# The feed-forward input projection of a decoder layer as seven products of quarters, with its gates passed through DRAM

## The chip, the cores and the metric

The kernel runs on one core of one Trainium2 chip. The metric is the device time of one execution in microseconds (us). Engines are named as in the profile: PE (TensorE) multiplies matrices, with its weight loads counted apart as PEld; DVE (VectorE) does element-wise work; ACT (ScalarE) casts and activation functions; POOL (GpSimd) element-wise work and DMA issues; SP (SyncE) only issues DMAs. Each engine works through its own instructions strictly in order.

## The reference

One layer of a decoder, 1024 tokens of width 1024, in float32. A token mixer (three branches, an output projection) comes first and is not touched. What matters here is the end:

```python
mix = hybrid_mixer(x, ...)                                  # ends in merged @ w_out
x = layer_norm(DEEPNORM_ALPHA * x + mix, ln1_g, ln1_b)
h1, h3 = split(x @ w_ffn_in, 2)                             # w_ffn_in: 1024 x 5632
ffn = (silu(h1) * h3) @ w_ffn_out                           # w_ffn_out: 2816 x 1024
x = layer_norm(DEEPNORM_ALPHA * x + ffn, ln2_g, ln2_b)
```

## The kernel before

Every float32 operand is held as two float32r parts, hi (a cast on ACT) and lo (the value minus hi, on DVE), and every product is three matmuls: hi by hi, hi by lo and lo by hi. A matmul has a 128x128 block of one operand stationary and 512 columns of the other moving, and adds into a bank of PSUM (`acc`, eight banks in this stage).

Weights come through `WeightStream` (`W`): a chunk of 512 KB is loaded by SP's queue into `w_raw` (L82, two buffers), split by ACT (`w_hi`, L96) and DVE (`w_lo`, L97; two buffers each) and used by a step of matmuls (L179). `W.run` emits the steps in order and yields after some matmuls; `run_steps` then runs one closure of the list `later`, so that norms and transposes are placed between matmuls. A scheduler sets the final order on each engine from what is emitted and its own estimates.

The output projection leaves the sums of a row tile (128 tokens) in PSUM; tiles 0 to 3 are done first, then 4 and 5, then 6 and 7. `ln1_front` adds the residual (`residual`, L914, DVE) and queues the norm: statistics (L924, L927 on DVE), a square root (L928, ACT), a reciprocal (L929), a scaling (L932) and the multiplication by ln_g (L935) on DVE, the addition of ln_b (L936) on POOL, and a store of the row to `x1_dram` on POOL's queue (L966), from which it is read again as the residual of the second norm (`res`, L908). Then come the transposes: `split_transpose` puts four 128x128 blocks of a row tile into PSUM by PE (L250), and ACT and DVE split them (L252, L253) into `x1h` and `x1l`, one pair of tiles for each half of the tokens.

The feed-forward goes over the halves of the tokens, `th` = 0 and 1. `ffn_in(th)` takes the 22 blocks j of 128 hidden columns; for each it projects h1 (columns j*128) and h3 (columns 2816 + j*128): 8 blocks of the contraction by 3 matmuls each. ACT takes the silu of h1 from PSUM (L990), DVE multiplies by h3 from PSUM (L995), and the gate is split into `gh` (L996, ACT) and `gl` (L997, DVE), which stay in SBUF. `ffn_out(th)` multiplies them with the output weights, for two halves of 512 columns and, for each, all 22 blocks j and 4 row tiles, 3 matmuls each; the second norm follows through `later`, so that the norm of th = 0 lies beside the projection of th = 1.

## Time and profile before

| what | value |
|---|---|
| three runs | 2314.52, 2318.84, 2319.31 us; median 2318.84 |
| span of the profiled execution | 2313.5 us; time around it isn't on the page, the median is 5.3 us above the span |
| busy | PE 98%, PEld 83%, DVE 54%, ACT 39%, POOL 12% of the span |
| output projection | until about 1571 us of the span |
| input projection, th = 0 and th = 1 | 1571 to 1814 and 1937 to 2180 us |
| output product, th = 0 and th = 1 | 1814 to 1937 and 2180 to 2304 us |

A row of a timeline gives the start, the time, the engine, the line of the kernel, the operation and out<-in; several like operations without a gap are one row with their count, and in brackets stands how long the engine was idle before and what ended that. A row of DMA issues gives the count, the size and the median time from issue to landing.

### The profile page before, as it was taken

How to read it: one execution, taken by the hardware profiler on the slowest of the kernel's cores; microseconds unless marked ns; L12 is line 12 of the kernel's file. 1: busy time of each engine (PE TensorE's matmuls, PEld its weight loads, DVE VectorE, ACT ScalarE, POOL GpSimd, SP SyncE). 2: the span in 40 equal slices, each digit the busy share in tenths (PEclk: the TensorE clock that was granted, in tenths of full speed). 3: DMA queues.
4: the chain of work that ended last, by engine and by line, in shares of the span. 5: the costliest groups of instructions: out<-in, count | busy, mean ns of one | idle time of the engine just before them, and what ended most of it. 6: DMA issues, size and time to landing. Idle time of an engine off the chain costs nothing.

```text
span 2313.5 us, 29381 instructions
## 1 busy us (share of the span) xinstructions
PE 2270.6 (98%) x11441; PEld 1919.2 (83%) x11441; DVE 1248.0 (54%) x2370; ACT 910.6 (39%) x1674; POOL 274.0 (12%) x267
## 2 busy tenths in 40 slices
PE   8989999999999999999999999999999999999998
PEld 6777888998888888788888888888888887888886
DVE  5789888777867778611232332475333226333335
ACT  4664766655656555511221221323232213323222
POOL 1332122212121222000000000021000002000001
PEclk9999999999999999999999999999999999999999
DMA  4123123122222233411231221343333334333333
GB/s 137 55 69 100 47 64 78 48 47 63 46 64 46 54 77 113 138 59 46 75 99 46 73 83 46 114 155 123 96 96 100 105 114 128 99 100 92 114 119 114
DMA packets 232651, 199.08 MB, mean 86 GB/s; under 512 B 8704, under 2 KB 196160, under 8 KB 232512
## 3 DMA queue, kind: packets, MB, share of 16 engines
q1 hardware_dynamic: 207360, 137.90, 19.7%
q0 software_dynamic: 10752, 32.03, 5.6%
q10 hardware_dynamic: 14400, 27.27, 3.6%
q8 instruction: 90, 1.47, 0.3%
q14 instruction: 49, 0.40, 0.1%
HBM read 161.52 MB, written 25.17 MB: 81 GB/s over the span
## 4 chain that ended last, share of the span: by engine, by line
PE 90%; DVE 6%; ACT 1%; issue 1%; DMA 1%; SPq 0%; DVEq 0%; ACTq 0%
PE acc L179 79%; PE o L179 4%; PE s L179 4%; PE pt L516 3%; DVE xc L359 1%; DVE w_lo L97 1%; DMA xin<-in_x_dram 0%; DVE xc L356 0%; PE pt L250 0%; DVE m L398 0%; DVE pt_l L521 0%; DVE r L932 0%; DVE p L557 0%; DVE gate L397 0%; DVE p L600 0%
## 5 line engine op out<-in xcount | busy, mean ns | idle before, releaser
L96 ACT CAST w_hi<-w_raw 128x1024 fp32r<-128x1024 f32 x233 | 245.2, 1052 | 797.3 <-PE acc L179 752.7
L97 DVE TENSOR_TENSOR w_lo<-w_raw,w_hi 128x1024 fp32r<-128x1024 f32 x195 | 248.0, 1272 | 492.4 <-ACT w_hi L96 488.3
L179 PE MATMUL acc<-xh,w_hi 128*128 128x512 f32 x1056 | 419.4, 397 | 5.0 <-DVE kl L501 2.0
L179 PE MATMUL acc<-xl,w_hi 128*128 128x512 f32 x1056 | 416.4, 394 | 0.0
L179 PE MATMUL acc<-xh,w_lo 128*128 128x512 f32 x1056 | 415.5, 393 | 0.0
L179 PE MATMUL acc<-x1h,w_lo 128*128 128x512 f32 x704 | 274.3, 390 | 2.7 <-DVE w_lo L97 2.7
L179 PE MATMUL acc<-x1h,w_hi 128*128 128x512 f32 x704 | 274.6, 390 | 0.0
L179 PE MATMUL acc<-x1l,w_hi 128*128 128x512 f32 x704 | 273.9, 389 | 0.0
L179 PEld LDWEIGHTS acc<-xh,w_hi 128*128 128x128 f32 x1056 | 199.7, 189 | 44.6 <-ACT xr L348 2.6
L179 PEld LDWEIGHTS acc<-xh,w_lo 128*128 128x128 f32 x1056 | 199.6, 189 | 39.3
L179 PEld LDWEIGHTS acc<-xl,w_hi 128*128 128x128 f32 x1056 | 200.0, 189 | 37.6
L936 POOL TENSOR_TENSOR r<-r,ln_b 128x1024 f32<-128x1024 f32 x15 | 40.6, 2714 | 1300.6 <-DVE r L935 1275.8
L520 ACT CAST pt_h<-pt 128x512 fp32r<-128x512 f32 (+3 forms) x256 | 124.9, 500 | 92.1 <-PE pt L516 87.2
L179 PEld LDWEIGHTS acc<-x1h,w_lo 128*128 128x128 f32 x704 | 132.1, 188 | 31.1 <-DVE w_lo L97 3.5
L521 DVE TENSOR_TENSOR pt_l<-pt,pt_h 128x512 fp32r<-128x512 f32 (+3 forms) x256 | 144.4, 572 | 19.7 <-ACT pt_h L520 17.5
L179 PEld LDWEIGHTS acc<-x1h,w_hi 128*128 128x128 f32 x704 | 132.2, 188 | 27.2
L179 PEld LDWEIGHTS acc<-x1l,w_hi 128*128 128x128 f32 x704 | 132.2, 188 | 27.1
L179 PE MATMUL acc<-yh,w_hi 128*128 128x512 f32 x384 | 149.4, 389 | 0.0
L179 PE MATMUL acc<-yl,w_hi 128*128 128x512 f32 x384 | 149.4, 389 | 0.0
L179 PE MATMUL acc<-yh,w_lo 128*128 128x512 f32 x384 | 149.4, 389 | 0.0
L516 PE MATMUL pt<-ident,p 128*128 128x128 f32 x816 | 128.3, 276 | 2.1 <-DVE pt_l L521 1.4
L179 PE MATMUL o<-pt_h,v 128*128 128x256 f32 (+1 forms) x464 | 117.4, 275 | 2.5 <-DVE yp L510 1.8
(278 smaller groups left out, 4069.4 us busy)
## 6 DMA issues: line engine op xcount, KB each, us to landing
w_raw<-in_w_ffn_in_dram SPq DMA_DIRECT2D x88, 512.0 KB, 3.6
w_raw<-in_w_in_dram SPq DMA_DIRECT2D x76, 512.0 KB, 3.7
w_raw<-in_w_ffn_out_dram SPq DMA_DIRECT2D x47, 512.0 KB, 3.6
w_raw<-in_w_branch_dram SPq DMA_DIRECT2D x24, 512.0 KB, 3.9
yraw<-y_dram ACTq DMA_DIRECT2D x48, 256.0 KB, 3.4
w_raw<-in_w_out_dram SPq DMA_DIRECT2D x12, 512.0 KB, 3.5
kh<-kh POOLq DMA_DIRECT2D x20, 256.0 KB, 5.9
kl<-kl POOLq DMA_DIRECT2D x20, 256.0 KB, 6.4
```

The source lines that it names most:

```text
L96: self.nc.scalar.copy(hi, raw)
L97: self.lo_engine.tensor_sub(lo, raw, hi.bitcast(F32))
L179: pe.matmul(o, a, b, start=start, stop=stop, skip_group_check=True)
L359: dve.scalar_tensor_tensor(xc, xr[:, 1 + j:1 + j + S], vec[:, j * 8 + ct:j * 8 + ct + 1], xc, op0=OP.mult, op1=OP.add)
L516: pe.transpose(pt[:, i * P:(i + 1) * P], b, ident)
L520: act.copy(dst_h, v)
L521: dve.tensor_sub(dst_l, v, dst_h.bitcast(F32))
L936: (pool if cols == D else dve).tensor_add(r[:, sl], r[:, sl], lnp["b"][:, sl])
```

## The change

The input projection is done by one level of Strassen's scheme (in Winograd's form). The activations are cut into four quarters, a00 and a01 (tokens 0 to 511; first and second half of the width), a10 and a11 (tokens 512 to 1023), and so are the weights of a block j: rows in two halves, columns h1 and h3. In place of eight products of quarters there are seven, of the operands a00, a01, a11 and the sums s1 = a10 + a11, s2 = s1 - a00, s3 = a00 - a10 and s4 = a01 - s2, with the weights' own quarters or their sums t1 to t4.

- `ln1_front` forms the activation sums on DVE for tiles 4 to 7 (L1000 to L1006), writing over the rows of the norm. The row's store to `x1_dram` is now issued by SP (L983); for tiles 6 and 7 DVE adds ln_b. `run_steps` runs two closures per piece from tile 4 on. Transposes: 112 in place of 64.
- `front_step` does the a00 and a01 products of the first four blocks (`NA` = 4), which need only tokens 0 to 511; the first result is copied out (`p1`), then a01's is added in the same bank and silu taken.
- `prep(j)` loads the two weight chunks of a block (L1083), forms t1 to t4 on POOL (`wsum`, L1088) and splits them, and one quarter, on ACT and DVE (`wsplit`, L1098 and L1099; the first chunk whole for j of 4 and above).
- `pair(j)` does the products of a block, for both halves of the tokens together: a00, s2, s1, s3, a01, s4, a11 in banks ba, bb, bc, bd; s4 goes on in bc and a11 in bd, after DVE has taken what stood there (L1154, L1158). DVE adds and multiplies to the two gates, which POOL's queue stores to `g_dram` (L1168, L1175).
- `load_g` reads the gates back, 22 for th = 0 on SP's queue and 22 for th = 1 on POOL's (L1203), and splits them for `ffn_out`, into the room of s2, s3 and s4 (j below 12) or new tiles. Both `ffn_out` follow each other; the norm of th = 0 lies beside `ffn_out(1)`.

The core of the diff:

```diff
-    def run_steps(g):
+    def run_steps(g, n=1):
         for _ in g:
-            if later:
-                later.pop(0)()
+            for _ in range(n):
+                if later:
+                    later.pop(0)()
...
-        halves, rest = norm_ops(r, D, lambda sl: pool.dma_start(x1_dram[tt], r))
+        halves, rest = norm_ops(r, D, lambda sl: sync.dma_start(x1_dram[tt], r), dve if tt >= 6 else pool)
...
+            def sums0():
+                s1 = lnr.tile([P, HALF], F32, tag="s1", bufs=4, name="s1")
+                rows_["s1", i] = s1
+                dve.tensor_add(s1, r[:, :HALF], r[:, HALF:])
+                dve.tensor_sub(r[:, :HALF], rows_[i][:, :HALF], r[:, :HALF])
+
+            def sums1():
+                lo, hi = rows_[i][:, :HALF], rows_[i][:, HALF:]
+                dve.tensor_sub(lo, rows_["s1", i], lo)
+                dve.tensor_sub(hi, hi, lo)
+            later.extend([sums0, sums1])
...
+    def product(bank, op, bh, bl, start):
+        ah, al = ops[op]
+        for k in range(4):
+            wh, wl = bh[:, k * P:(k + 1) * P], bl[:, k * P:(k + 1) * P]
+            mm(bank, wh, ah[:, k, :], start and k == 0, False)
+            mm(bank, wh, al[:, k, :], False, False)
+            mm(bank, wl, ah[:, k, :], False, k == 3)
...
+    def front_step(j):
+
+        def f(hi, lo):
+            bank = acc8.tile([P, HALF], F32, tag="acc", name="acc")
+            got = []
+            for q in range(2):
+                sl = slice(q * HALF, (q + 1) * HALF)
+                yield from product(bank, L_OPS[q], hi[:, sl], lo[:, sl], q == 0)
+                got.append(front_evac(bank, q))
+            front[j] = got
...
+    def wsum(j, n, a, b, op):
+        t = sring.tile([P, HALF], F32, tag="t", bufs=3, name="t")
+        pool.tensor_tensor(t, a, b, op=op)
+        raws[j, n] = t
...
+        def p1():
+            wsum(j, "t1", b(0, 1), b(0, 0), OP.subtract)
+            wsum(j, "t2", b(1, 1), raws[j, "t1"], OP.subtract)
...
+        def p5():
+            wsum(j, "t3", b(1, 1), b(0, 1), OP.subtract)
+            wsplit(j, "t3", raws[j, "t3"])
+        def p6():
+            wsplit(j, "b11", b(1, 1))
+            wsum(j, "t4", b(1, 0), raws[j, "t2"], OP.subtract)
+            wsplit(j, "t4", raws[j, "t4"])
...
+        yield from product(bb, "s2", *parts.pop((j, "t2")), True)
+        u2 = temp()
+        dve.tensor_add(u2, p1, bb)
+        yield from product(bc, "s1", *parts.pop((j, "t1")), True)
+        v = temp()
+        dve.tensor_add(v, u2, bc)
+        yield from product(bd, "s3", *parts.pop((j, "t3")), True)
+        dve.tensor_add(v, v, bd)
+        if j >= NA:
+            yield from product(ba, "a01", b0h[:, HALF:], b0l[:, HALF:], False)
+            silu = front_evac(ba, 1)
+        yield from product(bc, "s4", *parts.pop((j, "b11")), False)
+        g = temp()
+        dve.tensor_add(g, u2, bc)
+        dve.tensor_mul(g, g, silu)
+        pool.dma_start(g_dram[0, j], g)
+        yield from product(bd, "a11", *parts.pop((j, "t4")), False)
+        g = temp()
+        dve.tensor_add(g, u2, bd)
+        act.activation(g, g, AF.Silu)
+        dve.tensor_mul(g, g, v)
+        pool.dma_start(g_dram[1, j], g)
...
+    def load_g(th, j):
...
+        raw = l.bitcast(F32)
+        (pool if th else sync).dma_start(raw, g_dram[th, j])
+        act.copy(h, raw)
+        dve.tensor_sub(l, raw, h.bitcast(F32))
...
+    for f in prep(0):
+        f()
+    for j in range(HT):
+        nxt = prep(j + 1) if j + 1 < HT else []
+        drain(pair(j, lambda n: nxt[n]() if nxt else None))
+    srS.close()
+    for j in range(12):
+        load_g(0, j)
```

The order on the engines, before and after. On DVE, from the last norm work on tile 5 to the residual of tile 6; before:

```order
L932 TENSOR_SCALAR r<-r,sm 128x1024
L935 TENSOR_TENSOR r<-r,ln_g 128x1024
L914 SCALAR_TENSOR_TENSOR r<-res,acc 128x512 x2
L924 BN_STATS stats<-r 128x6
L914 SCALAR_TENSOR_TENSOR r<-res,acc 128x512
L924 BN_STATS stats<-r 128x6 x2
L914 SCALAR_TENSOR_TENSOR r<-res,acc 128x512
L927 BN_AGGR sm<-stats 128x2
L924 BN_STATS stats<-r 128x6
```

After (`s_...` is a tile's s1, `r<-r` at L1001 and L1006 a sum written over a row):

```order
L939 TENSOR_TENSOR r<-r,ln_g 128x1024
L1001 TENSOR_TENSOR r<-r 128x512
L1000 TENSOR_TENSOR s_13891<-r 128x512
L1005 TENSOR_TENSOR r<-s_13857,r 128x512
L1006 TENSOR_TENSOR r<-r 128x512
L1001 TENSOR_TENSOR r<-r 128x512
L1005 TENSOR_TENSOR r<-s_13891,r 128x512
L1006 TENSOR_TENSOR r<-r 128x512
L918 SCALAR_TENSOR_TENSOR r<-res,acc 128x512 x2
L928 BN_STATS stats<-r 128x6
L918 SCALAR_TENSOR_TENSOR r<-res,acc 128x512
L928 BN_STATS stats<-r 128x6 x2
```

Seven sums of tiles 4 and 5, and one more above the piece, now stand ahead of the residual of tile 6 (L918).

On PE, from the output projection (`wo_h`, `mh`) on; before, all of the projection of the first half follows:

```order
L179 MATMUL acc<-wo_h,mh 128x512 x2
L179 MATMUL acc<-wo_l,mh 128x512 x2
L179 MATMUL acc<-wo_h,ml 128x512 x2
L179 MATMUL acc<-x1h,w_hi 128x512
L179 MATMUL acc<-x1l,w_hi 128x512
L179 MATMUL acc<-x1h,w_lo 128x512
L179 MATMUL acc<-x1h,w_hi 128x512
```

After, the same place is followed by the front products (`oph` and `opl` are the parts of a00, a01, a11 or s1), and their end by the last transposes and pair 0, whose weight parts are called `ph` and `pl`:

```order
L180 MATMUL acc<-oph,w_lo 128x512
L180 MATMUL acc<-oph,w_hi 128x512
L180 MATMUL acc<-opl,w_hi 128x512
L180 MATMUL acc<-oph,w_lo 128x512
L251 MATMUL pt<-ident,r 128x128 x14
L180 MATMUL acc<-s2h,ph 128x512
L180 MATMUL acc<-s2l,ph 128x512
L180 MATMUL acc<-oph,ph 128x512
L180 MATMUL acc<-opl,ph 128x512
L180 MATMUL acc<-s2h,pl 128x512
L180 MATMUL acc<-s2h,ph 128x512
L180 MATMUL acc<-s2l,ph 128x512
```

The first pair's s2 product now stands behind transposes of sums of all eight row tiles.

On DVE inside the projection; before, a block j and half:

```order
L97 TENSOR_TENSOR w_lo<-w_raw,w_hi 128x1024
L995 TENSOR_TENSOR silu<-silu,acc 128x512
L97 TENSOR_TENSOR w_lo<-w_raw,w_hi 128x1024
L997 TENSOR_TENSOR gl<-silu,gh 128x512
L97 TENSOR_TENSOR w_lo<-w_raw,w_hi 128x1024
L995 TENSOR_TENSOR silu<-silu,acc 128x512
L97 TENSOR_TENSOR w_lo<-w_raw,w_hi 128x1024
```

After, one whole pair of the steady stretch (`e` are the terms of the gates):

```order
L1099 TENSOR_TENSOR pl<-t,ph 128x512
L1154 TENSOR_TENSOR e<-e,acc 128x512
L1099 TENSOR_TENSOR pl<-w_raw,ph 128x512
L1158 TENSOR_TENSOR e<-e,acc 128x512
L1099 TENSOR_TENSOR pl<-t,ph 128x512
L1099 TENSOR_TENSOR w_lo<-w_raw,w_hi 128x1024
L1166 TENSOR_TENSOR e<-e,acc 128x512
L1099 TENSOR_TENSOR pl<-t,ph 128x512
L1167 TENSOR_TENSOR e<-e,silu 128x512
L1172 TENSOR_TENSOR e<-e,acc 128x512
L1099 TENSOR_TENSOR pl<-t,ph 128x512
L1174 TENSOR_TENSOR e<-e 128x512
```

Twelve operations of 512 columns and one of 1024 per pair, with the adds that free a bank (L1154, L1158) between the splits.

On POOL, which did nothing in the projection before but the last adds and stores of the first norm:

```order
L936 TENSOR_TENSOR r<-r,ln_b 128x1024
L966 DMA x_dram<-r 128x1024
L936 TENSOR_TENSOR r<-r,ln_b 128x1024
L966 DMA x_dram<-r 128x1024
L936 TENSOR_TENSOR r<-r,ln_b 128x1024 x7
```

After, in the middle of the projection:

```order
L1088 TENSOR_TENSOR t<-w_raw,t 128x512
L1175 DMA g_dram<-e 128x512
L1088 TENSOR_TENSOR t<-w_raw 128x512
L1088 TENSOR_TENSOR t<-w_raw,t 128x512
L1088 TENSOR_TENSOR t<-w_raw 128x512
L1168 DMA g_dram<-e 128x512
L1088 TENSOR_TENSOR t<-w_raw,t 128x512
L1175 DMA g_dram<-e 128x512
L1088 TENSOR_TENSOR t<-w_raw 128x512
L1088 TENSOR_TENSOR t<-w_raw,t 128x512
L1088 TENSOR_TENSOR t<-w_raw 128x512
L1168 DMA g_dram<-e 128x512
```

The weight sums of a later block stand between the stores of the gates, in one queue.

On SP, from the output projection's weights on; before:

```order
L82 DMA w_raw<-in_w_out_dram 128x1024 x12
L82 DMA w_raw<-in_w_ffn_in_dram 128x8x128 x44
L82 DMA w_raw<-in_w_ffn_out_dram 128x2x512 x22
L82 DMA w_raw<-in_w_ffn_in_dram 128x8x128 x4
L1053 DMA out_dram<-r 128x1024
L82 DMA w_raw<-in_w_ffn_in_dram 128x8x128
```

After:

```order
L82 DMA w_raw<-in_w_out_dram 128x1024 x12
L983 DMA x_dram<-r 128x1024
L82 DMA w_raw<-in_w_ffn_in_dram 128x8x128 x2
L983 DMA x_dram<-r 128x1024 x3
L82 DMA w_raw<-in_w_ffn_in_dram 128x8x128 x2
L983 DMA x_dram<-r 128x1024 x3
L1083 DMA w_raw<-in_w_ffn_in_dram 128x8x128
L983 DMA x_dram<-r 128x1024
L1083 DMA w_raw<-in_w_ffn_in_dram 128x8x128 x43
L82 DMA w_raw<-in_w_ffn_out_dram 128x2x512 x3
L1203 DMA gl<-g_dram 128x512 x12
L82 DMA w_raw<-in_w_ffn_out_dram 128x2x512
L1203 DMA gl<-g_dram 128x512 x10
```

Stores of the first norm stand between weight loads; three loads for the output product, then twelve loads of gates, one weight load, and ten more gates.

## The prediction

> **What bounds the kernel now.** I read the engines' busy shares first, then the chain that ended last, then the windows of each stage.

> ```profile
> PE 2270.6 (98%) x11441; PEld 1919.2 (83%) x11441; DVE 1248.0 (54%) x2370; ACT 910.6 (39%) x1674; POOL 274.0 (12%) x267
> PE 90%; DVE 6%; ACT 1%; issue 1%; DMA 1%; SPq 0%; DVEq 0%; ACTq 0%
> ...
> 1571.00:1814.00 243.00, 243.00 (x1089) 201.15 (x1088) 95.68 (x107) 74.82 (x97) 6.38 (x4) 1.00 0.35 105
> ...
> 1937.30:2180.00 242.70, 240.03 (x1058) 198.09 (x1057) 99.77 (x108) 75.94 (x95) 11.62 (x4) 1.00 0.36 107
> ...
> 1620.00:1800.00 180.00, 180.00 (x796) 149.05 (x795) 62.23 (x68) 52.61 (x66) 0.00 (x0) 1.00 0.33 97
> 1820.00:1930.00 110.00, 110.00 (x473) 88.53 (x473) 29.50 (x28) 21.06 (x20) 0.00 (x0) 1.00 0.32 101
> ```

> TensorE (PE) carries 90% of the chain. The rows with a colon are windows: sum of time, then busy time and count of PE, weight loads, DVE, ACT, POOL, then granted clock, DMA share and GB/s. The first two windows are the two passes of the input projection (one per token half): PE is busy throughout, DVE 39 to 41%. So here a matmul taken away is time taken away, as long as DVE, ACT, POOL and the transfers keep up with a shorter stage. 180 us / 796 = 0.2261 us per matmul in the projection, 110 / 473 = 0.2326 in the output product.

> **Matmuls removed.** Before: 22 tiles x 2 column halves x 2 token halves x 24 = 2112. After: 22 pairs x 7 products x 12 = 1848. 264 x 0.2261 = 59.7 us, all on the path: **-59.7**. Shapes are unchanged (weights stationary, 512 tokens moving), so I keep 0.2261.

> **Transposes added.** 64 become 112.

> ```profile
> 1606.71 0.40 PE L179 MATMUL acc<-x1h,w_lo 128*128 128x512 f32 x1
> 1606.95 0.60 PE L250 MATMUL pt<-ident,r 128*128 128x128 f32 x4
> 1607.30 0.48 PE L179 MATMUL acc<-x1h,w_hi 128*128 128x512 f32 x1
> ```

> Four transposes widen the step between two matmuls from 0.23 to 0.59 us: 0.09 each. 48 x 0.09 = **+4.3**.

> **The passage from output projection to the first full pair.** Before, the stage started with tokens 0-511 and left tiles 6 and 7 until later. After, only products with a00 and a01 can run without them: four pairs x 24 = 96 matmuls, 21.7 us, and the 80 transposes beside them, 7.2 us. The first s2 product needs the norms of tiles 6 and 7, the operand sums, all splits and DVE's first weight split.

> ```profile
> 1544.80 1.88 DVE L253 TENSOR_TENSOR x1l<-pt,x1h 128x512 fp32r<-128x512 f32 x3
> ...
> 1560.85 0.81 DVE L932 TENSOR_SCALAR r<-r,sm 128x1024 f32<-128x1024 f32 x1
> 1561.70 1.22 DVE L935 TENSOR_TENSOR r<-r,ln_g 128x1024 f32<-128x1024 f32 x1
> 1569.71 1.29 DVE L914 SCALAR_TENSOR_TENSOR r<-res,acc 128x512 f32<-128x512 f32 x2 [6.78 <-PE acc L179]
> ...
> 1948.85 2.33 DVE L935 TENSOR_TENSOR r<-r,ln_g 128x1024 f32<-128x1024 f32 x2
> ...
> 1554.26 2.40 POOL L936 TENSOR_TENSOR r<-r,ln_b 128x1024 f32<-128x1024 f32 x1 [5.84 <-PE acc L179]
> ...
> 1563.07 2.41 POOL L936 TENSOR_TENSOR r<-r,ln_b 128x1024 f32<-128x1024 f32 x1 [5.54 <-issue]
> ...
> x_dram<-r POOLq DMA_DIRECT2D x8, 512.0 KB, 3.9
> res<-x_dram ACTq DMA_DIRECT2D x16, 256.0 KB, 3.2
> ```

> Back to back a 512-wide DVE operation costs 0.60 us (1.88 for three, the last one 0.68), a 1024-wide one 1.14 (2.33 for two). From the residual of tile 6 to that first weight split DVE has 4 residual adds, 4 statistics, 20 splits of transposes, 8 operand sums and 1 weight split of 512 (37 x 0.60 = 22.2), 2 scalings (2 x 0.73), 2 multiplications, 2 additions and 2 weight splits of 1024 (6 x 1.14 = 6.8) and small ones (0.5): 31.0 us. When does it start? The sums of tiles 4 and 5 write over rows whose store must have landed, and the stores now stand on SP's queue, in order between weight loads that wait for their room in the ring; the last POOL add ends at 1565.5, its store 3.9 later, three sums 1.8: 1571.2, about 1.5 us after the 1569.71 of before. 1571.2 + 31.0 = 1602.2. POOL's first three weight sums (below) can hold DVE 3 x 1.2: 1605.8. PE has work from 1571.0 for 28.9 us: until 1599.9. Bubble: **+6** (ends 0, if the store is early and the sums are in a gap, and 14, if splits also wait for their transposes and casts).

> ```profile
> 950.00:958.00 8.00, 6.61 (x32) 5.87 (x33) 3.83 (x8) 2.35 (x5) 1.62 (x3) 0.79 0.20 69
> 1952.00:1958.00 6.00, 3.33 (x15) 2.43 (x14) 6.00 (x4) 3.34 (x4) 4.22 (x2) 1.00 0.22 89
> ```

> In the first of these windows, behind thin PE work, the granted clock is 0.79: 8 x 0.21 = 1.7 us lost. In the second, with one wait of 3 us, it stays 1.00. The passage is like the first: **+1.7** (ends 0 and 4).

> [...]

> **The pairs.** A pair's PE time is 7 x 12 x 0.2261 = 19.0 us; for the first four, whose a00 and a01 products are done, 5 x 12 x 0.2261 = 13.6. Beside it DVE has 5 weight splits and 7 gate operations of 512 and one split of 1024: 12 x 0.60 + 1.14 = 8.3 (7.2 in the first four). POOL has four sums of 512 and two DMA issues. No row shows a POOL operation of that width; the nearest is 2.40 for 1024 columns. Half is 1.2 (ends 1.2 and 2.4). What POOL does to DVE:

> ```profile
> 1950.19 6.03 POOL L936 TENSOR_TENSOR r<-r,ln_b 128x1024 f32<-128x1024 f32 x2 [3.02 <-DVE r L935]
> ...
> 1951.11 2.89 DVE L932 TENSOR_SCALAR r<-r,sm 128x1024 f32<-128x1024 f32 x1
> 1953.92 0.68 DVE L995 TENSOR_TENSOR silu<-silu,acc 128x512 f32<-128x512 f32 x1
> 1954.52 2.78 DVE L97 TENSOR_TENSOR w_lo<-w_raw,w_hi 128x1024 fp32r<-128x1024 f32 x1
> ...
> 1957.36 0.50 PE L179 MATMUL acc<-x1h,w_lo 128*128 128x512 f32 x1 [2.67 <-DVE w_lo L97]
> ```

> Beside two POOL adds the scaling took 2.89 instead of 0.81 and the split 2.78 instead of 1.22: DVE stands while POOL adds. The multiplication from PSUM between them took its usual 0.68. So I add POOL's time to DVE's: 8.3 + 4 x 1.2 = 13.1 of 19.0, and 7.2 + 4.8 = 12.0 of 13.6. Hidden by PE, at a thin margin in the first four pairs. ACT has 6 casts, a copy and 2 gates, about 5 us. The wait that comes nearer is that of the products that go on in a bank: s4 needs the add of bank bc, a11 that of bd, each with one product (2.7 us) of other PE work between, in the steady pairs two (5.4). Behind the splits queued on DVE that can fail: **+2** in all (ends 0, and 22 x 1.2 = 26, one POOL sum exposed per pair).

> [...]

> **The passage of the gates through DRAM.** 44 stores on POOL's queue and 44 loads (22 on SP's, 22 on POOL's) of 256 KB are about 23 MB in some 800 us, at a DMA share of 0.35. What can cost time is the seam: after pair 21 its gate must be stored (at most 3.9) and read back (3.2), then cast and split (1.3): 8.4 us. But the output product takes the 22 row blocks in order, 12 matmuls x 0.2326 = 2.8 us each: the last is wanted 58 us after the first. Blocks 0 to 3 wait only for the room of s2, free 14 us before the end. SP's first three weight loads of the stage stand ahead of the 12 gate loads; the fourth stands behind them and is wanted 16.7 us after the start, while the last of the 12 rooms (s4) comes free 2.7 us before it. **+0.5** (ends 0 and 15). The cast and the split of each gate are those of before, moved behind its load.

> **The norm beside the second output product.** On POOL the 22 gate loads of the second half stand ahead of the norm's adds; the last of them waits for the last use of its room, the end of the first half's product, when the norm's turn comes too: nothing. Before, tiles 0 to 3 of the last norm lay beside the second projection and cost the 3.06 us hole that ends at 1957.36. After, they lie beside the output product of the second half, whose weight chunks last 5.6 us; the third chunk's split stands behind three multiplications and POOL adds on DVE. The cover is alike, so is the hole, at about 5.8: **+2.7** (ends -3 and 6).

> **Sum.** -59.7 + 4.3 + 6 + 1.7 + 2 + 0.5 + 2.7 = -42.5. The profiled execution spans 2313.5 us; the page shows no time around it, and the median of the three runs is 5.3 above. 2313.5 - 42.5 = 2271.0; against the median 2318.8 - 42.5 = **2276**.

> **The rivals.**
> - POOL's sums reach PE. For: every sum sits in front of a split that a product waits for, and POOL also issues the stores in order, so a sum stands behind a store whose gate isn't ready. Against: preparation runs about a pair and a half ahead. One sum exposed per pair, 22 x 1.2 = 26 less the 2 counted: **2300**.
> - The round trip is exposed at the seam: 8.4 for the gates and as much again if the fourth weight chunk stands behind them in SP's queue: **2293**.
> - PE's rhythm is that of the output product: 1848 x (0.2326 - 0.2261) = 12: **2288**. For: banks change every 12 matmuls, four times as many operands. Against: the shapes are the old ones.
> - Slower: preparation loses its lead, and one operand per pair is made just in time: sum 1.2, cast 0.6, split 0.7 in series, 2.5, or 22 x 2.5 = 55: 2276 + 55 = **2331**. It decides from 42.5 / 22 = 1.9 us per pair. For: the three buffers of sums and POOL's strict order. Against: 6 us of DVE time to spare in 18 of the 22 pairs; with sums of 2.4 us DVE would have 17.9 of 19.0.

> **How the numbers follow.** My forecast (2264 to 2284) 0.50; POOL's sums 0.16; seam 0.12; rhythm 0.08; slower 0.07; better than forecast 0.07 (no bubble: -59.7 + 4.3 = -55.4, 2263). The range leaves out the slower case and the upper half of the POOL case: 2263 to 2303. Differences of under 0.2%, 4.6 us, can hardly be told from none here. Only the slower case and the space toward it make no gain: faster 0.91, same 0.02, slower 0.07.

> **What the profile after would show.** Right: PE's count 264 - 48 = 216 lower at 0.226 per matmul; one bubble of some 6 us before the first s2 product, ended by a DVE split; DVE about 70% busy in the pairs, with splits stretched beside POOL; pairs 19 us apart. Wrong: PE waits for gate adds or splits in every pair; pairs 20 us or more apart; a hole of over 5 us where the output product starts, ended by a gate load; a clock below 1.00 in the pairs.

## The result and the profile after

The changed kernel takes 2276.8 us (median of 4 runs, 2274.9 to 2278.7), the one before 2316.7 (4 runs, 2313.6 to 2319.3): ratio 0.983, interval 0.9816 to 0.9844, 39.9 us less. The forecast was 2276. The sum came out; several of its terms did not, and they cancelled. The median before is now that of four runs, 2.2 us under the 2318.8 that the forecast started from. The spans of the two profiled executions differ by the same 39.9 us (2313.5 and 2273.6), so each term can be measured.

The page after, its first line and the engines of the chain:

```profile
PE 2223.5 (98%) x11225; PEld 1874.8 (82%) x11225; DVE 1339.3 (59%) x2554; ACT 923.0 (41%) x1748; POOL 439.9 (19%) x411
PE 87%; DVE 8%; ACT 2%; issue 2%; DMA 1%; POOL 0%; SPq 0%; DVEq 0%; POOLq 0%; ACTq 0%
```

The windows that answer to those of before, with the same columns: the passage, the first pairs, the rest of the pairs, then a steady stretch of pairs and one of the output product.

```profile
1571.00:1604.67 33.67, 32.06 (x182) 27.24 (x181) 31.58 (x49) 18.83 (x35) 4.54 (x3) 1.00 0.31 102
1604.67:1664.00 59.33, 56.17 (x237) 43.77 (x238) 37.95 (x50) 15.85 (x27) 26.60 (x23) 1.00 0.34 106
1664.00:2011.80 347.80, 347.80 (x1516) 284.25 (x1515) 175.37 (x241) 108.09 (x167) 128.36 (x104) 1.00 0.29 90
1700.00:1900.00 200.00, 200.00 (x873) 163.48 (x872) 99.44 (x137) 61.19 (x94) 81.21 (x65) 1.00 0.26 81
...
2020.00:2130.00 110.00, 110.00 (x473) 88.57 (x472) 46.61 (x56) 36.63 (x48) 10.14 (x19) 1.00 0.54 172
```

PE is still the bound, with 216 instructions fewer. But in the steady stretch 873 matmuls take 200 us, 0.2291 each, where the projection before had 0.2261 (180 us for 796). The starts of the matmuls, with the rows below, give the account (a step is the time from one start to the next); "forecast" is the term on record.

| term | forecast | measured | from |
|---|---|---|---|
| 264 matmuls fewer | -59.7 | -59.8 | 264 x 0.2266, the step between two starts in the projection before |
| 48 transposes more | +4.3 | +5.2 | passage 32.5 us, less 96 matmuls and the hole: 9.1; 80 stand in the passage, and the 32 in the same stage of the kernel before cost 3.9 |
| hole before the first s2 product, lower clock behind it | +7.7 | +1.7 | wait of 1.6 us at 1604.67, clock 1.00 |
| waits in the pairs | +2 | +4.5 | four waits from 1617 to 1662 and the steps of 0.34 behind them |
| slower step of the matmuls | 0 | +5.9 | 1752 matmuls in 407.4 us less the waits, against 0.2266 |
| seam to the output product | +0.5 | 0 | one piece of the chain from 1662 to 2141 |
| norm beside the output product | +2.7 | +0.8 | hole 3.6 us, before 2.8 in the projection |
| start of the stage, end of the kernel, rest | 0 | +1.8 | stage starts 1.1 later, last norm ends 1.2 later, -0.5 |
| sum | -42.5 | -39.9 | |

The waits, from the timeline of PE (in brackets the idle time before and its releaser; the row of 1631.49, the first s2 product of pair 2, has none):

```profile
1604.67 0.50 PE L180 MATMUL acc<-s2h,ph 128*128 128x512 f32 x1 [1.61 <-ACT ph L1098]
...
1617.48 0.51 PE L180 MATMUL acc<-s2h,ph 128*128 128x512 f32 x1 [1.28 <-ACT ph L1098]
...
1631.49 0.39 PE L180 MATMUL acc<-s2h,ph 128*128 128x512 f32 x1
...
1643.25 0.50 PE L180 MATMUL acc<-s2h,ph 128*128 128x512 f32 x1 [0.49 <-ACT ph L1098]
...
1647.89 0.50 PE L180 MATMUL acc<-s4h,ph 128*128 128x512 f32 x1 [0.70 <-DVE e L1154]
...
1662.21 0.50 PE L180 MATMUL acc<-s4h,ph 128*128 128x512 f32 x1 [0.69 <-DVE e L1154]
```

The chain of work through the first pairs (start, time, what):

```profile
1622.01 4.92 DMA w_raw<-in_w_ffn_in_dram
...
1627.10 1.29 POOL t L1088
...
1630.90 1.28 DVE pl L1099 x2
...
1634.95 4.77 DMA w_raw<-in_w_ffn_in_dram
...
1662.21 478.82 PE acc L180 x2075
```

The chain names what my sum had no term for: in the first pairs it runs through the weight loads. The two raw buffers hold just one pair; the next load starts when the last split has read them, lands 4.7 to 4.9 us later, and sums, casts and splits follow, about 13 us a round (12.8, 12.9 and 13.5 us between the starts of the loads). A short pair has 13.6 us of products, so the round alone wouldn't make PE wait; but PE's order puts the next pair's first s2 matmuls ahead of the last product of the pair at hand. From 1604.67 to 1617.48 and from 1631.49 to 1643.25 PE starts 48 matmuls, 11 us of work, and then waits; from 1617.48 to 1631.49 it starts 60, 14 us, and doesn't. The two waits of 0.7 us are those of s4 for the add that takes bank bc (L1154), which stands on DVE behind splits of the same round. A steady pair of 19 us hides the round, and from 1662 to 2141 PE waits for nothing, across the seam at 2012 too.

The passage, on DVE, with the hole in the output product behind it (DVE and POOL):

```profile
1566.90 0.69 DVE L1001 TENSOR_TENSOR r<-r 128x512 f32<-128x512 f32 x1 [3.26 <-DMA x_dram<-r]
...
1571.50 1.28 DVE L918 SCALAR_TENSOR_TENSOR r<-res,acc 128x512 f32<-128x512 f32 x2
...
1605.07 1.89 DVE L1099 TENSOR_TENSOR pl<-t,ph 128x512 fp32r<-128x512 f32 x3
...
2150.35 2.89 DVE L936 TENSOR_SCALAR r<-r,sm 128x1024 f32<-128x1024 f32 x1
2153.17 3.35 DVE L97 TENSOR_TENSOR w_lo<-w_raw,w_hi 128x1024 fp32r<-128x1024 f32 x1
...
2148.19 10.59 POOL L940 TENSOR_TENSOR r<-r,ln_b 128x1024 f32<-128x1024 f32 x3 [11.93 <-DVE sm L933]
```

The residual of tile 6 started at 1571.5 (forecast 1571.2), behind a store that had to land, as said; but it was the store of the first of the two rows, with seven sums behind it, where the forecast had the second's and three. The first weight split started at 1605.1 (forecast 1605.2, 0.6 ahead of the 1605.8).

### The profile page after: what moved, and what is told of

Its sections match the earlier page's. It is cut to its first block, busy times and chain, and to the rows that moved or that the text cites. A ratio compares the mean times of both kernels' runs of the same rounds, so it can differ in the third digit from the quotient of the medians.

```text
span 2273.6 us, 29553 instructions
## 1 busy us (share of the span) xinstructions
PE 2223.5 (98%) x11225; PEld 1874.8 (82%) x11225; DVE 1339.3 (59%) x2554; ACT 923.0 (41%) x1748; POOL 439.9 (19%) x411
## 4 chain that ended last, share of the span: by engine, by line
PE 87%; DVE 8%; ACT 2%; issue 2%; DMA 1%; POOL 0%; SPq 0%; DVEq 0%; POOLq 0%; ACTq 0%
PE acc L180 74%; PE o L180 4%; PE s L180 4%; PE pt L517 4%; DVE xc L360 1%; DMA w_raw<-in_w_ffn_in_dram 1%; DVE pl L1099 1%; DVE w_lo L97 1%; PE pt L251 1%; DVE r L939 1%; POOL t L1088 0%; DVE xc L357 0%; DVE r L936 0%; DMA xin<-in_x_dram 0%; DVE m L399 0%
## 5 line engine op out<-in xcount | busy, mean ns | idle before, releaser
L96 ACT CAST w_hi<-w_raw 128x1024 fp32r<-128x1024 f32 x149 | 156.6, 1051 | 440.6 <-PE acc L180 404.5
L97 DVE TENSOR_TENSOR w_lo<-w_raw,w_hi 128x1024 fp32r<-128x1024 f32 x111 | 141.2, 1272 | 297.2 <-ACT w_hi L96 297.2
L512 POOL DMA_DIRECT2D y_dram<-yp x96 | 52.2, 544 | 424.6 <-DVE yp L511 325.4
L180 PE MATMUL acc<-w_lo,gh 128*128 128x512 f32 x288 | 114.1, 396 | 4.2 <-DVE w_lo L97 4.2
L1098 ACT CAST ph<-t 128x512 fp32r<-128x512 f32 x88 | 53.9, 622 | 156.7 <-PE acc L180 84.3
L180 PE MATMUL o<-pt_l,v 128*128 128x256 f32 (+1 forms) x464 | 113.6, 285 | 1.8 <-DVE pt_l L522 1.8
L604 ACT ACTIVATE p<-p,small 128x128 f32<-128x128 f32 (+7 forms) x128 | 99.5, 777 | 38.0 <-DVE small L601 36.6
L180 PE MATMUL acc<-w_hi,gl 128*128 128x512 f32 x288 | 113.9, 395 | 0.0
## 6 DMA issues: line engine op xcount, KB each, us to landing
w_raw<-in_w_in_dram SPq DMA_DIRECT2D x76, 512.0 KB, 3.9
w_raw<-in_w_ffn_in_dram SPq DMA_DIRECT2D x48, 512.0 KB, 4.5
w_raw<-in_w_ffn_out_dram SPq DMA_DIRECT2D x47, 512.0 KB, 3.7
w_raw<-in_w_branch_dram SPq DMA_DIRECT2D x24, 512.0 KB, 3.9
yraw<-y_dram ACTq DMA_DIRECT2D x48, 256.0 KB, 3.3
g_dram<-e POOLq DMA_DIRECT2D x44, 256.0 KB, 3.5
w_raw<-in_w_out_dram SPq DMA_DIRECT2D x12, 512.0 KB, 3.6
gl<-g_dram SPq DMA_DIRECT2D x22, 256.0 KB, 4.0
```

Source lines behind the costliest of these rows:

```text
L96: self.nc.scalar.copy(hi, raw)
L97: self.lo_engine.tensor_sub(lo, raw, hi.bitcast(F32))
L180: pe.matmul(o, a, b, start=start, stop=stop, skip_group_check=True)
L512: pool.dma_start(dst, yp[:, :n])
L604: act.activation(p[:, :n], p[:, :n], AF.Exp, bias=m, scale=-1.0, accum_out=sm[:, 1:2])
L1098: act.copy(hi, src)
```

## The experiments

My theory after the result: the pairs' waits come from the loop of the weight loads (L), not from POOL holding DVE (P); the passage is set by DVE's chain, which the front products cover (D); and the slower step of the matmuls is a matter of where the operands stand in SBUF, not of the products' shortness. A single run says little of a few microseconds: the profiled executions of the change and of those of its variants that leave addresses as they were reach the passage anywhere between 1569.4 and 1574.5 us. So variants with one run are read from their windows and rows.

**Where the operands stand.** In before and after, the step follows the operands: products with a00 and a01 up front and the projection before go at 0.2266, those with s2, s3, s4 at about 0.229, those of a pair with a11 and s1 and the output product at about 0.233. In the first kind both operands start at a multiple of 256 bytes, in the second both start 32 bytes off one, in the third one of them does. First try: 32 bytes on either side.

```diff
-    epsc = ff1.tile([P, 1], F32, name="epsc")
+    epsc = ff1.tile([P, 16], F32, name="epsc")[:, 0:1]
...
+    frp.tile([P, 8], F32, tag="pad", name="pad")
```

> The changed kernel with 32 bytes of padding on either side of SBUF, so that the addresses of the operands s2, s3, s4, of the weight parts ph and pl, of the gates and of the output projection's weights become multiples of 64 bytes (they stood at 32 past one). Nothing else changes. Theory A (the pitch of a matmul depends on whether its two operands stand at the same offset from 64 bytes: both at 0 gives 0.2266 us, both at 32 gives 0.229, one of each 0.233): every stage goes to 0.2266; 528 x 0.0059 + 792 x 0.0022 in the pairs, 1056 x 0.0066 in the output product, 288 x 0.0065 in the output projection = 3.1 + 1.7 + 7.0 + 1.9 = about 13.7 us less, 2263. Theory B (stationary operands outside the first 41 KB of SBUF are slower, wherever they start): pitches as before, 0.229 to 0.234, time unchanged within 0.2%. Theory C (twelve matmuls per bank and four times as many operands slow the rhythm): the output product, which has long runs, keeps 0.2326 and so do the pairs.

> The kernel before with 32 bytes of padding ahead of the gates, so that they and the output projection's weights start at a multiple of 64 bytes. Theory A: output product 1056 x 0.0064 = 6.8 and output projection 1.9 us less, 8.7 us in all (about 2310 against 2318.8); the input projection stays at 0.2266. Theory B: no change within 0.2%.

Theory A fell: 2276.0 us (ratio to before 0.9826, 0.981 to 0.9843) against 2276.8, and the kernel before 2315.4 (0.9994, 0.9985 to 1.0004). But B and C fell with it, for single steps moved by up to 4 ns, in both directions: a11 and s1 from 0.2335 to 0.231, s2 to s4 from 0.229 to 0.231 to 0.233, the output projection before from 0.233 to 0.229; only the output product stayed.

```profile
1700.00:1900.00 200.00, 200.00 (x870) 163.32 (x869) 99.34 (x136) 61.17 (x94) 81.51 (x65) 1.00 0.25 81
2020.00:2130.00 110.00, 110.00 (x473) 88.64 (x472) 46.65 (x56) 36.19 (x47) 10.15 (x19) 1.00 0.53 170
```

These windows of the padded kernel show the same steady rates (870 and 473). Second try: 224 bytes on either side, so that every operand stands at a multiple of 256.

```diff
-    epsc = ff1.tile([P, 1], F32, name="epsc")
+    epsc = ff1.tile([P, 64], F32, name="epsc")[:, 0:1]
...
+    frp.tile([P, 56], F32, tag="pad", name="pad")
```

> The changed kernel with 224 bytes of padding on either side of SBUF, so that all operands of the matmuls named at the first padding start at a multiple of 256 bytes. With 32 bytes of padding the pitches moved both ways (products with s2, s3, s4 from 0.229 to 0.231-0.233, a11 and s1 from 0.2335 to 0.231, output product the same 0.233); in all runs so far, matmuls whose two operands start at multiples of 256 go at 0.2266 to 0.2275. Theory A2 (both operands must start at a multiple of 256 bytes): 0.2266 to 0.2275 in the pairs and in the output product: about 13 us less than 2276.8, 2264. Rival F (the placement matters in a way that no common alignment cures; what is fast is the first 41 KB for the stationary operand): the mean pitch stays between 0.229 and 0.233, time within 0.2% of 2276.8.

> The kernel before with 224 bytes of padding ahead of the gates. Theory A2: the output product goes from 0.2326 to 0.227 per matmul (1056 x 0.006 = 6 us) and the output projection by 1.9: about 8 us less than 2316.6. Rival F: output product unchanged, at most the 1 us in the output projection that 32 bytes brought; within 0.2%.

2266.2 us (ratio to before 0.9785, 0.9768 to 0.9801), 10.6 less than the change; the kernel before with the first of the two paddings 2307.1 (0.9963, 0.995 to 0.9976), 9 less. The same windows of the changed kernel so padded:

```profile
1700.00:1900.00 200.00, 200.00 (x884) 165.62 (x883) 100.24 (x138) 61.87 (x95) 80.18 (x65) 1.00 0.26 84
2020.00:2130.00 110.00, 110.00 (x487) 91.10 (x486) 50.29 (x62) 36.72 (x46) 11.73 (x22) 1.00 0.55 174
```

The output product of the kernel before, padded:

```profile
1820.00:1930.00 110.00, 110.00 (x487) 91.10 (x486) 31.26 (x31) 21.10 (x20) 0.00 (x0) 1.00 0.36 109
```

884 in 200 us and 487 in 110: 0.226 in every stage. So the slower step was neither the seven products' fault nor the output product's own rhythm: it was placement. The gain is 2.4 us short of the 13 expected. In the profiled execution the hole in the output product was 0.25 us longer than in the change, and 15 matmuls behind it went at half clock, 3 us (shown at the end); and the passage took 35.0 us in place of 32.5, as PE now waited 2.3 us for one of DVE's sums.

**The waits of the first pairs.** Pairs 1 to 3 work on pair 0's weights:

```diff
+        if 0 < j < NA:
+            raws[j] = raws[0]
+            return
```

> The changed kernel, but pairs 1 to 3 don't load weights: they work on those of pair 0 (six loads of 512 KB left out, sums, splits and products all kept). Theory L (the waits in the first four pairs come from the weight loads: the two raw buffers hold one pair, so a load starts only when the last split of the pair before has read them, and lands 4.5 to 4.9 us later): the waits at the starts of pairs 1 to 3 and the two behind L1154 go, about 4.5 us, pairs 0 to 3 take 4 x 13.6 = 54.5 to 55 us from first to last product. Theory P (POOL's sums hold DVE): the waits stay, 59 us.

2271.8 us in one run. The window from the first s2 product on, against 237 matmuls in 59.33 us above:

```profile
1604.40:1664.00 59.60, 59.59 (x258) 48.19 (x259) 41.53 (x54) 19.81 (x32) 32.02 (x26) 1.00 0.20 62
```

The waits are gone, with POOL's sums all there; the pairs end 4.5 us earlier (402.9 in place of 407.4 from first start to the output product). The loads belong to the cause; holding by POOL doesn't suffice. The other half, the sums on DVE:

```diff
-        pool.tensor_tensor(t, a, b, op=op)
+        dve.tensor_tensor(t, a, b, op=op)
```

> The changed kernel with the sums of the weights on DVE in place of POOL (88 operations of 512 columns, 0.60 us on DVE in place of 1.3 to 1.6 on POOL). Theory P (POOL's sums hold DVE, and that is what the pairs wait for): all waits in the first four pairs go, as in the run with the same weights, about 4.5 us. Theory L (the weight loads' loop): the loop of load, two or three sums, casts and splits becomes shorter by about 2 x 0.7 per pair, so the waits shrink by about 3 us in all but the load stays in the chain; the steady pairs stay at the same length in both.

2277.0 us in one run, as the change. All waits behind pair 0 are gone here too, more than L's 3 us, so load and sums were in series, and taking out either is enough. What each is worth alone these two runs don't say, for the scheduler set the products of the first pairs in another order in both; and another order by itself wasn't run. The gain was spent at pair 0: its sums now stand on DVE among the last splits, as the chain of work shows,

```profile
1605.99 0.68 DVE t L1088
1606.67 0.60 DVE s4l L254
1607.27 0.60 DVE opl L254
1607.87 0.61 DVE t L1088
```

and PE waits longer for them, here in its timeline, with half clock behind (steps of 0.43 us):

```profile
1609.17 0.80 PE L180 MATMUL acc<-s2h,ph 128*128 128x512 f32 x1 [3.41 <-ACT ph L1098]
```

Third, the same work with earlier last reads of the raw weights:

```diff
-        t = sring.tile([P, HALF], F32, tag="t", bufs=3, name="t")
+        t = sring.tile([P, HALF], F32, tag="t", bufs=4, name="t")
...
-        return sring.tile([P, HALF], F32, tag="e", bufs=6, name="e")
+        return sring.tile([P, HALF], F32, tag="e", bufs=5, name="e")
...
         def p1():
+            wsplit(j, "b11", b(1, 1))
```

(and the split of b11 taken out of `p6`)

> The changed kernel with the same work, but the last reads of a pair's raw weights come earlier: a fourth buffer for the sums t (one fewer for the gates' terms), so that t4 needn't wait for the split of t2, and the split of the quarter b11 ahead of the sums. Theory L (a serial loop per pair: load of 4.9 us, sums on POOL, casts and splits, then the next load; 13 to 14.3 us in the first four pairs against 13.6 us of products) gives load 4.9 + four sums 5.2 = about 10 to 11 us per pair, under 13.6: the waits of pairs 1 to 3 go, 3 to 4.5 us from first to last product of the pairs. If only the holding of DVE by POOL counts, which is unchanged here, the waits stay.

2280.3 us in one run, 3.5 more than the change; from the first s2 product to the output product 410.5 us, against 407.4. The rounds did shorten: the loads in the chain of work stand 10.7 us apart, then 11.6 and 11.2, and pairs 1 to 3 wait for nothing.

```profile
1606.29 4.53 DMA w_raw<-in_w_ffn_in_dram
...
1616.98 4.86 DMA w_raw<-in_w_ffn_in_dram
...
1628.58 5.39 DMA w_raw<-in_w_ffn_in_dram
...
1639.81 4.34 DMA w_raw<-in_w_ffn_in_dram
```

But b11 is wanted last and now stands first in the queues of ACT and DVE: pair 0's first weight parts come later (waits of 2.6 and 1.2 us) and pair 4 waits, with half clock behind the waits of pair 0 (mean granted clock 0.989, against 0.993 in the change). L's loop is confirmed, my cure for it wasn't one.

**The passage.** Two pairs up front in place of four:

```diff
-    NA = 4
+    NA = 2
```

> The changed kernel with two pairs' a00 and a01 products up front in place of four (48 matmuls, 10.9 us, move from the passage into pairs 2 and 3, which become steady ones). Theory D (the first s2 product waits for a chain of DVE and ACT work that the front products only cover): it starts at the same time after the output projection's end (32.8 us) or up to 1.5 us earlier, since the splits and evacuations of two pairs fall away; the hole grows from 1.7 to 11 or 12 us, less 2 us of waits in pairs 2 and 3 that the longer pairs hide: 7 to 9 us slower, about 2285. Theory E (PE's own work in the passage sets its length, the hole is a constant delay of casts): the passage shortens by 10.9 us, the pairs lengthen by as much, time as after.

2286.1 us in one run, 9.3 more than the change, where D said about 2285 and E no change. PE's waits in the passage:

```profile
1587.80 0.63 PE L251 MATMUL pt<-ident,r 128*128 128x128 f32 x4 [1.60 <-DVE r L1005]
1592.76 1.08 PE L251 MATMUL pt<-ident,r 128*128 128x128 f32 x4 [4.33 <-DVE r L1005]
...
1600.40 0.50 PE L180 MATMUL acc<-s2h,ph 128*128 128x512 f32 x1 [1.35 <-DVE opl L254]
```

PE now waits for DVE's sums. The first s2 product came 30.0 us after the output projection's last matmul, in place of 32.8: 2.8 earlier, not at most 1.5. Two weight splits of 1.14 us left DVE's chain; the other 0.5 stays open. The waits are 7.3 us, not 11 or 12, and part of the 9.3 is something else: 15 matmuls behind the hole in the output product went at half clock, 3 us, which the profiled execution of the change didn't have.

So with two pairs D holds. With four, D's chain and its cover are about equally long, and the last link is E's: the chain of work of the change lies on PE through the passage, then on ACT's casts and the splits behind them.

```profile
1598.75 2.79 PE acc L180 x12
...
1601.56 0.60 ACT silu L1050
1602.16 0.49 ACT s4h L253
...
1602.67 1.29 DVE s4l L254 x2
```

**The hole in the output product.** ln_b of the second norm's tiles 0 to 3 on DVE:

```diff
-                                  dve if tt == KT - 1 else pool)
+                                  pool if 4 <= tt < KT - 1 else dve)
```

> The changed kernel with the addition of ln_b of the second norm's first four tiles on DVE in place of POOL (tiles 4 to 6 stay on POOL). Theory: the hole of 3.6 us in the output product of the second half comes from POOL's adds, which hold the scaling (2.89 in place of 0.81) and the weight split (3.35 in place of 1.22): with three adds of 1.14 on DVE instead, of which not all stand ahead of the split, the hole shrinks to under 1.5 us, and the half clock behind it goes: 2 to 4 us less. Rival: the split is late because it stands behind the norm's work on DVE whatever runs beside it: the hole stays at 3 to 4.

2271.1 us in one run, 5.7 less than the change. DVE at the place of the two rows of 2150 and 2153 above:

```profile
2150.34 0.81 DVE L936 TENSOR_SCALAR r<-r,sm 128x1024 f32<-128x1024 f32 x1
2151.06 1.22 DVE L97 TENSOR_TENSOR w_lo<-w_raw,w_hi 128x1024 fp32r<-128x1024 f32 x1
```

2.89 and 3.35 became 0.81 and 1.22, although an add of 1.22 now stands ahead of them, and the step at this place fell from 3.81 to 0.57 us: 3.2 us. The rest of the 5.7 isn't shown to be the edit's: in this execution the passage began 2.7 us earlier than in the change, ahead of anything that the edit touches.

**Together.** All three parts; the kernel before with the two that apply to it; and the two that had helped:

> The changed kernel with all three: operands at multiples of 256 bytes, ln_b of the second norm's first four tiles on DVE, the shorter loop of the weights. If the three are independent: 2266.2 (256 bytes) less 3.2 for the hole in the output product and up to 3 for the half clock behind it, less 4 for the pairs' waits: 2256 to 2259. If they hide each other (an earlier pair only waits longer later): not under 2261.

> The kernel before with the two parts that apply to it: operands at multiples of 256 bytes and ln_b of the second norm's first four tiles on DVE. 2307.05 less the 3.1 and 0.7 us of waits and some 1.5 us of half clock that stand in the second projection: 2302 to 2305. Against it, the seven products should keep a gain of 45 to 48 us: 59.8 of matmuls less transposes, passage and waits.

> The changed kernel with operands at multiples of 256 bytes and ln_b of the second norm's first four tiles on DVE, without the reordering of the weights' loop (whose two runs moved the waits from pairs 1 to 3 to the starts of pairs 0 and 4 and added half-clock stretches). If the two parts are independent: 2266.2 less 3.2 to 3.6 for the hole and up to 3 for the half clock behind it, 2260 to 2263. If the saving on the norm is lost elsewhere: 2265 to 2267.

| kernel | us | ratio to before, interval |
|---|---|---|
| change + 256 bytes + norm + shorter loop | 2265.4 | 0.9779, 0.9762 to 0.9795 |
| before + 256 bytes + norm | 2302.2 | 0.9938, 0.9923 to 0.9953 |
| change + 256 bytes + norm | 2260.2 | 0.9762, 0.9745 to 0.9779 |

The first missed its 2256 to 2259 and fell where its rival had it, not under 2261: against the third, the reordering costs 5 us here, with waits of 2.6 and 1.6 us at pair 0, 2.7 and 1.2 at pair 4 and half clock behind both (steps of 0.43 from 1607.1 us on; a granted clock of 0.83 from 1643 to 1653). The third met its 2260 to 2263 and beats both kernels, by 16.6 and 55.5 us. Against the kernel before with the same two repairs the seven products are worth about 42 us, under the 45 to 48 expected: their passage and waits remain.

## Why the prediction was right

- **Matmuls removed** (-59.7): right to 0.1 us. PE was the bound, and stayed it with the pairs at 19 us.
- **The passage** (+6 and +1.7): the prediction was right that DVE's chain starts behind a store that must land, and that it is about as long as its cover; with two pairs fewer up front PE waits for it. With four the last link was another one. PE worked without a wait until 1603.1, not 1599.9, since the stage began 1.1 us later and the 80 transposes took 9.1 us, not 7.2; then 1.6 us of casts followed, and what ended the hole was ACT's cast of the first weight part (L1098), ahead of the DVE split that the prediction named. That the split came at the time forecast was in part luck: POOL's sums held DVE by 1.0 us (a sum at 1595.97 took 1.65 in place of 0.69), not 3.6, and DVE stood idle for 2.0 us, 1.5 of it for ACT's cast of s4. The lower clock of the +1.7 didn't come in this execution: it was 1.00 in the passage and in the first pairs.
- **The pairs** (+2, measured 4.5): this step failed. It added POOL's holding to DVE's time and compared 12.0 with 13.6; what the waits came from was the loop through the raw buffers, which the sum left out, and an order of the products that put only 48 matmuls, 11 us, beside it. The order of SP showed loads, not when their room comes free. Two of the four waits, behind L1154, are of the kind that the +2 was meant for, but they too are gone in the run without the loads of pairs 1 to 3. In the steady pairs DVE was busy for 50% (175.37 of 347.80 us), not 70%. The holding itself is real: the rows of 2.89 and 3.35 became 0.81 and 1.22 without POOL's adds. Not every DVE operation beside a POOL sum was held: beside one that began at 1653.56 the add from PSUM took 0.68, and the multiplication of two SBUF tiles behind it 1.19, where it took 0.68 on average in the steady pairs (timelines of DVE and POOL after).

```profile
1653.50 0.68 DVE L1166 TENSOR_TENSOR e<-e,acc 128x512 f32<-128x512 f32 x1
1654.22 1.19 DVE L1167 TENSOR_TENSOR e<-e,silu 128x512 f32<-128x512 f32 x1
...
1653.56 1.29 POOL L1088 TENSOR_TENSOR t<-w_raw 128x512 f32<-128x512 f32 x1 [6.37 <-DMA w_raw<-in_w_ffn_in_dram]
```

- **The step of the matmuls**: I kept 0.2261 "since shapes are unchanged" and priced the rival at 12 us with a chance of 0.08. It came in at half that price (5.9), for another reason than the one I gave it (banks and operands): placement. The row of 0.2326 for the output product was the hint; I took it for a property of that product. The transposes came to 0.11 us each, not 0.09.
- **The seam** (+0.5): right, nothing. **The norm** (+2.7): the hole was there, from the cause named, but 3.6 us long and not 5.8.
- **The rivals**: the DRAM round trip is hidden; PE isn't held up in each pair; preparation keeps its lead in the steady ones.

So 2276 was met by luck. 6.0 us too much for the passage, 1.9 for the norm and 0.5 for the seam stood against 8.4 too little for pairs and step, 0.9 for the transposes and 1.8 for the ends; that leaves a gain 2.6 us smaller than forecast, and the median that it is taken from fell by 2.2 us with the fourth run. The range held for better reasons than the point: the matmuls removed, and PE as the bound.

## What to carry to other kernels

Look up how many bundles of operands the raw buffers hold: where it is one, load, preparation and last read form a loop, and whether a stage hides it depends on how much work the order of the instructions leaves between one first use and the next. Measure the step between matmuls stage by stage; where the same shape runs at two rates, look at the addresses before the algorithm. And check a forecast term by term: a right sum says little of its terms.

## What was not expected of the hardware

The half clock (a granted clock of 0.50) didn't follow the length of a hole. In each of the traces the granted clock changes only at times that lie a multiple of 3.41 us apart, so the windows below are cut at those times; the first number behind a window's times is its length, the second PE's busy time, the third from the right the granted clock. The change, behind its step of 3.81 us in the output product:

```profile
2151.58:2154.99 3.41, 1.58 (x7) 0.94 (x5) 3.41 (x2) 1.05 (x1) 3.41 (x2) 1.00 0.37 154
2154.99:2158.40 3.41, 1.82 (x8) 1.51 (x9) 3.41 (x2) 0.00 (x0) 3.41 (x2) 1.00 0.09 13
```

The change padded by 32 bytes, behind a step of 3.80 at the same place:

```profile
2153.21:2156.62 3.41, 0.12 (x1) 0.00 (x0) 3.41 (x3) 0.27 (x1) 3.41 (x2) 1.00 0.37 154
2156.62:2160.03 3.41, 3.30 (x8) 2.63 (x9) 3.41 (x3) 0.00 (x0) 2.28 (x1) 0.50 0.56 119
```

The change with the norm on DVE, behind a step of 2.30 at the start of pair 1:

```profile
1613.87:1617.29 3.42, 1.51 (x7) 0.82 (x6) 0.69 (x1) 1.25 (x3) 3.20 (x3) 1.00 0.00 0
1617.29:1620.70 3.41, 3.41 (x10) 2.63 (x10) 3.41 (x5) 1.65 (x3) 1.60 (x1) 0.50 0.02 5
```

The first hole lies across two windows, in which PE was still busy for 1.58 and 1.82 us, and the clock stayed; the second, as long, fills one, and the next went at half clock; in the third PE was busy for 1.51 us of one window, and the clock halved too. In all 14 traces, from 200 us on, a window at full clock in which PE was busy for at most 0.44 of the time was followed by one at half clock, 28 times of 28; over 0.59 it never was; between the two it was 9 times of 29 (in before and in the change once each, the windows from 949.64 and 950.09 us, both with 0.58). So in these traces the clock went with the work done in such a window, and a hole of 2 to 4 us costs or doesn't by where it falls; what decides between 0.44 and 0.59 isn't shown. This is why holes of nearly equal length cost up to 3 us more in one execution than in another (15 matmuls at 0.427 in place of 0.227, in the kernel padded to 256 bytes).
